# GLA layer of a two-layer trunk: gates, keys and queries projected ahead of the recurrence by the seven-product block scheme

## The chip, the cores and the metric

The kernel runs on one core of a Trainium2 chip. The metric is the device time of one execution in microseconds. The matmuls of the projections run on TensorE (PE); the other engines of the core are VectorE (DVE), ScalarE (ACT), GpSimd (POOL) and SyncE (SP), and SP's queue issues the DMAs.

## The reference

A sequence of 1024 tokens with 1024 features goes through two layers. Each has a token mixer and a SwiGLU channel mixer, both behind an RMS norm that is scaled and shifted by the conditioning vector. Layer 0 mixes by forgetting attention, layer 1 by gated linear attention (GLA), which the change is about:

```python
proj = h @ w_in                      # 1024 -> 512 q, 512 k, 1024 v, 1024 r, 16 a_lr
log_alpha = log_sigmoid(a_lr @ w_a2 + b_a) / 16
b = cumsum(log_alpha) within a chunk of 64
q_in, k_in, k_dec = q * exp(b), k * exp(-b), k * exp(b_last - b)
o_intra = tril(q_in @ k_in.T) @ v    # within the chunk
S_next = exp(b_last) * S + k_dec.T @ v
o = rms_norm(o_intra + q_in @ S) * g_o * silu(r)
y = o @ w_out
```

There are 4 heads with 128 key and 256 value features each.

## The kernel before, in words

Activations lie transposed, 128 features by 1024 tokens in a tile, in two halves of 512 tokens. A product in fp32 is three matmuls: a value is split into a rounded upper half (`split`, L163, a cast on ACT) and the rest (L164, a subtraction on DVE), and `mm3` (L241 to L243) adds upper by upper, upper by lower and lower by upper. So 128 output features of one half of the tokens cost 8 x 3 = 24 matmuls of 128x512.

The channel mixer of layer 0 doesn't multiply so. It takes weights and activations in 2 x 2 blocks and uses seven products of sums of blocks where the plain way has eight (`prod`, L1308; the sums of the products by `add`, L1317 to L1319, on DVE). Activation blocks are called B11, B12, B21, B22 and the sums T1 to T4; weight blocks are loaded and split by `op_block` and its companions (L693 and on), sums of weight blocks are made on POOL (L708, L710).

The GLA layer of before is plain. `norm_half` (L549) makes the normed activations h1. For head 0 the gate's rank-16 product and the values come first (`a_body`, `gv_body`). Then for each head `head_front` (L1693) projects keys (gk) and queries (gqp), multiplies them straight out of the matmul's accumulator by exponentials of the gate's running sum (`gate_exps`, L1675 to L1681) and splits them. `gate_ahead` (L1649) runs inside it: it makes the gate of the next head, with the scan of L1645 on DVE, and stores it in `gsum_d`. `head_back` (L1748) is the recurrence: scores in blocks (`intra`, masked at L1759 and split), the state (`state`: kv on PE, the step Sf at L1775 on DVE, its split S_t on ACT and DVE), the output go, its norm (sums of squares on ACT, L1818; gss on DVE and POOL; on_t at L1825), the transposes ogt and the product with the gate r (gs, L1788). `r_proj` (L1829) projects the head's gate r (gr, four tiles of 24 matmuls, silu at L1837 on ACT) and is woven into the recurrence. After it come the values of the next head. Heads 0 to 2 store their outputs to `og_d`; they are loaded again and split (gr, ghh, ghl), and the output product `out_chunk` (tiles go00xp) runs on them.

Weights come through one list of loads in the order of use (`feed`). Between all this `ada1` slips pieces of the conditioning product (POOL L381, ACT L379) in by a pace.

The program is written in one order, and a list scheduler with its own timeline then decides the order on each engine, by when it thinks operands and buffers ready. Names such as `weave(a, 13.0, b, 20.8)` only set the order in which it is given the work.

## Time and profile before

| what | us |
|---|---|
| three runs | 2418.40, 2418.31, 2414.46 |
| median | 2418.31 |
| profiled execution, first to last instruction (span) | 2415.5 |
| of it PE busy | 2373.4 |
| DVE busy | 1672.9 |
| ACT busy | 1191.8 |
| POOL busy | 1203.4 |

The profile tells no time of its own execution besides the span, which lies 1.0 us above the lowest and 2.9 us below the highest of the three runs. A group's row has its line, engine, operation, output and input, shapes and count, then busy time and the mean of one in ns, then the idle time of its engine just ahead of it and what ended that. A row of the timeline has start and duration, and in brackets the idle time ahead and its releaser.

### The profile page before, as it was taken

Reading aid. Unit: us, or ns where it says so; the run is one execution under the profiler, and the core shown is the slowest. Engines: PE = TensorE matmul, PEld = TensorE weight load, DVE = VectorE, ACT = ScalarE, POOL = GpSimd, SP = SyncE. Lnnn points to the kernel's source line nnn. Section 1 sums busy time; section 2 is a strip of 40 time slices with the busy share of each in tenths; the row PEclk is TensorE's granted clock in tenths of the full one; section 3 lists DMA queues with packets and bytes.
Section 4 is the critical chain, followed back from the end, with each engine's and each line's share of the span. In section 5 each row is a group of like instructions: output and inputs, shape, how many; then the busy total and the mean of one; then the engine's idle time right before and its main releaser. Section 6 shows DMA issues by size and latency. Waiting matters only on the chain.

```text
span 2415.5 us, 36053 instructions
## 1 busy us (share of the span) xinstructions
PE 2373.4 (98%) x12342; PEld 2018.3 (84%) x12342; DVE 1672.9 (69%) x2789; ACT 1191.8 (49%) x2288; POOL 1203.4 (50%) x1071
## 2 busy tenths in 40 slices
PE   7999999999999999999999999999999999999998
PEld 6788888878888888888888888898888888888888
DVE  6577677676687877876787545435586767675787
ACT  4665555675544444445324856654343333345325
POOL 4343344432347878853263646662335656653262
PEclk9999999999999999999999999999999999999999
DMA  9233333123335555457665334434325444347664
GB/s 272 72 106 114 100 111 105 62 97 114 127 103 178 184 172 174 155 187 260 228 201 171 89 110 126 135 124 154 114 85 172 164 133 151 133 174 256 232 202 148
DMA packets 329359, 361.88 MB, mean 150 GB/s; under 512 B 24460, under 2 KB 252968, under 8 KB 329176
## 3 DMA queue, kind: packets, MB, share of 16 engines
q1 hardware_dynamic: 328984, 359.57, 45.4%
q8 instruction: 97, 1.59, 0.3%
q14 instruction: 86, 0.70, 0.1%
q10 hardware_dynamic: 192, 0.02, 0.0%
HBM read 269.25 MB, written 90.24 MB: 149 GB/s over the span
## 4 chain that ended last, share of the span: by engine, by line
PE 82%; DVE 5%; DMA 4%; ACT 3%; issue 2%; POOL 2%; SPq 1%; DVEq 0%; POOLq 0%; ACTq 0%
PE p_b L243 16%; PE p_b L241 16%; PE p_b L242 16%; PE o_b L979 2%; PE t_b L965 2%; PE qk_b L241 2%; PE qk_b L243 2%; PE qk_b L242 2%; PE s_b L934 1%; PE s_b L935 1%; PE gr_b L243 1%; PE gr_b L242 1%; PE gr_b L241 1%; PE vps_b L241 1%; PE vps_b L242 1%
## 5 line engine op out<-in xcount | busy, mean ns | idle before, releaser
L164 DVE TENSOR_TENSOR o_s<-xv_s,o_s 128x512 fp32r<-128x512 f32 (+1 forms) x376 | 341.4, 911 | 78.4 <-ACT o_s L163 77.5
L163 ACT CAST o_s<-xv_s 128x512 fp32r<-128x512 f32 (+1 forms) x376 | 217.8, 587 | 320.3 <-PE p_b L243 254.4
L242 PE MATMUL p_b<-B,o_s 128*128 128x512 f32 x608 | 238.1, 392 | 0.0
L243 PE MATMUL p_b<-B,o_s 128*128 128x512 f32 x608 | 237.7, 391 | 0.0
L241 PE MATMUL p_b<-B,o_s 128*128 128x512 f32 x608 | 236.2, 391 | 0.0
L945 POOL TENSOR_SCALAR lp_s<-lp_s,st 128x128 f32<-128x128 f32 (+7 forms) x128 | 98.1, 771 | 265.7 <-DVE st L944 214.7
L708 POOL TENSOR_TENSOR ex_s<-xv_s,xv_s 128x512 f32<-128x512 f32 (+1 forms) x64 | 89.1, 1393 | 261.5 <-DMA xv_s<-in_ffn_w_in_dram 97.1
L241 PE MATMUL p_b<-T,o_s 128*128 128x512 f32 x480 | 186.7, 389 | 0.0
L242 PE MATMUL p_b<-T,o_s 128*128 128x512 f32 x480 | 186.7, 389 | 0.0
L243 PE MATMUL p_b<-T,o_s 128*128 128x512 f32 x480 | 180.7, 389 | 0.0
L243 PEld LDWEIGHTS p_b<-B,o_s 128*128 128x128 f32 x608 | 114.7, 189 | 23.9
L241 PEld LDWEIGHTS p_b<-B,o_s 128*128 128x128 f32 x608 | 114.7, 189 | 23.8
L242 PEld LDWEIGHTS p_b<-B,o_s 128*128 128x128 f32 x608 | 114.7, 189 | 23.7
L943 ACT ACTIVATE lp_s<-lp_s,st 128x128 f32<-128x128 f32 (+7 forms) x128 | 99.3, 777 | 61.1 <-DVE st L939 58.7
L381 POOL TENSOR_TENSOR ad_s<-ad_s,ad_s 128x512 f32<-128x512 f32 x62 | 89.4, 1442 | 54.0 <-ACT ad_s L379 29.6
L163 ACT CAST pt_s<-t_b 128x512 fp32r<-128x512 f32 (+1 forms) x160 | 79.6, 547 | 73.5 <-PE t_b L965 72.8
L710 POOL TENSOR_TENSOR xv_s<-ex_s,xv_s 128x512 f32<-128x512 f32 (+1 forms) x64 | 84.9, 1327 | 57.3 <-DVE o_s L164 55.1
L1319 DVE TENSOR_TENSOR ex_s<-ex_s,p_b 128x512 f32<-128x512 f32 x140 | 94.0, 680 | 27.0 <-PE p_b L243 26.9
L164 DVE TENSOR_TENSOR pt_s<-t_b,pt_s 128x512 fp32r<-128x512 f32 (+1 forms) x160 | 96.8, 631 | 13.2 <-ACT pt_s L163 12.9
L243 PEld LDWEIGHTS p_b<-T,o_s 128*128 128x128 f32 x480 | 90.1, 188 | 18.7
L241 PEld LDWEIGHTS p_b<-T,o_s 128*128 128x128 f32 x480 | 90.1, 188 | 18.7
L242 PEld LDWEIGHTS p_b<-T,o_s 128*128 128x128 f32 x480 | 90.1, 188 | 18.7
(1952 smaller groups left out, 7505.7 us busy)
## 6 DMA issues: line engine op xcount, KB each, us to landing
xv_s<-in_ffn_w_in_dram SPq DMA_DIRECT2D x176, 256.0 KB, 3.0
hid_B<-x SPq DMA_DIRECT2D x70, 512.0 KB, 2.7
ad_s<-in_ada_w_dram SPq DMA_DIRECT2D x384, 64.0 KB, 1.9
hid_T<-x SPq DMA_DIRECT2D x36, 512.0 KB, 2.8
xv_s<-in_ffn_w_out_dram SPq DMA_DIRECT2D x96, 192.0 KB, 4.1
ada_s<-in_ada_w_dram SPq DMA_DIRECT2D x128, 128.0 KB, 2.6
xv_s<-in_ffn_w_out_dram SPq DMA_DIRECT2D x40, 256.0 KB, 2.8
T2o<-hid_T SPq DMA_DIRECT2D x18, 512.0 KB, 9.0
```

The costliest lines, as they stand in the source:

```text
L163: nc.scalar.copy(hi, src)
L164: nc.vector.tensor_sub(lo, src, hi.bitcast(F32))
L241: nc.tensor.matmul(ps, ah, bh, start=start, stop=False)
L242: nc.tensor.matmul(ps, ah, bl, start=False, stop=False)
L243: nc.tensor.matmul(ps, al, bh, start=False, stop=stop)
L381: nc.gpsimd.tensor_add(acc, acc, raw)
L708: nc.gpsimd.tensor_add(s1, a21, a22)
L710: nc.gpsimd.tensor_sub(a11, s1, a11)
L943: nc.scalar.activation(lp, lp, AF.Exp, bias=mcur, scale=-1.0, accum_out=st[:, qi, 2:3])
L945: nc.gpsimd.tensor_scalar(lp, lp, st[:, qi, 3:4], 1.0, op0=ALU.mult, op1=ALU.mult)
L965: nc.tensor.transpose(tp[:, i, :], lps[qi][:, psl(2 * b + jj)], ident)
L1319: nc.vector.tensor_add(d, d if src is None else dest(G, src), ps)
```

## The change

The first layer's scheme is taken to the second layer's projections. Seven groups of two column blocks each, head 0's key and query, then for heads 1 to 3 the two gate blocks and the key and query, are projected ahead of the recurrence of all heads, each by seven products of 12 matmuls. Head 0's gate is projected plainly before them. The norm makes the blocks B and T (`g_norm`, `g_split`). A group's products are joined by `GroupRun`, one copy on ACT and seven additions on DVE; gates get their silu from SBUF; the results go to DRAM (`gs_d` for gates, `qk_d` for keys and queries). The gates' scans of all four heads run beside the groups. In the recurrence the value projection of the next head (`gv`, 64 steps of three matmuls) takes the gate's place beside `head_back`, 32 steps in it and 32 behind it; the last head has `out_chunk` there. `Front` loads running sums, keys and queries from DRAM, and multiplies and splits them; the lower halves of queries are now made on POOL. Outputs of heads 0 to 2 are loaded again ahead of head 3's recurrence.

```diff
+    GCOLS = {"r": lambda h: (2048 + 2 * h * P, 2048 + (2 * h + 1) * P),
+             "k": lambda h: (512 + h * P, h * P)}
...
+    GSEQ = [("r", 0), ("k", 0), ("r", 1), ("k", 1), ("r", 2), ("k", 2), ("r", 3), ("k", 3)]
...
-    loads += v_loads(Wg, 1024) + [(load_w16, Wg[:, 3072:3088], "aw")]
+    loads += gla_loads()
     for h in range(4):
-        if h:
-            loads += [a + (ws, 4) for a in v_loads(Wg, 1024 + h * 256)]
-        qk_ = [a + (ws, 4) for c0 in (512, 0) for a in w_loads(Wg, c0 + h * P)]
-        r_ = [a + (ws, 4) for i in range(2) for a in w_loads(Wg, 2048 + (2 * h + i) * P)]
-        loads += qk_ + r_ if h else r_[:1] + qk_ + r_[1:]
+        loads += [x_ + (ws, 4) for x_ in v_loads(Wg, 1024 + h * 256)]
...
+    y11, y21, y12, y22 = gya[:4], gya[4:], gy2[:4], gy2[4:]
+    g_block("T1", b_sl[4:8])
+    g_block("T2", b_sl[0:4])
+    g_block("T3", x_slots[0:4])
+    for k in range(4):
+        even = k % 2 == 0
+        nc.gpsimd.tensor_sub(y11[k], y12[k], y11[k])
+        g_split(gb["T1"][k], y11[k], 0)
+        nc.vector.tensor_sub(y11[k], y22[k], y11[k])
+        g_split(gb["T2"][k], y11[k], k, mcol(1, 0, k + 4) if even else None)
+    for k in range(4):
+        nc.gpsimd.tensor_sub(y12[k], y22[k], y12[k])
+        g_split(gb["T3"][k], y12[k], k, gds[:, k:k + 1] if k % 2 == 0 else None)
+    g_block("T4", hid_sl)
+    for k in range(4):
+        (nc.gpsimd if k % 2 else nc.vector).tensor_sub(y21[k], y21[k], y11[k])
+        g_split(gb["T4"][k], y21[k], 0)
...
+    def g_prod(nm_):
+
+        w, t = feed.next(), gb[nm_]
+        ps = pin([P, HALF], F32, f"gp{nm_}")
+        for k in range(4):
+            mm3(ps, w.hi[:, k, :], w.lo[:, k, :], t[k][:, 0], t[k][:, 1], k == 0, k == 3)
+        ada1(2.56)
+        return ps
...
+        OPS = ((("B11",), lambda c, p: nc.scalar.copy(c["11"], p["B11"])),
+               (("T2",), lambda c, p: nc.vector.tensor_add(c["12"], c["11"], p["T2"])),
+               (("B21",), lambda c, p: nc.vector.tensor_add(c["11"], c["11"], p["B21"])),
+               (("T3",), lambda c, p: nc.vector.tensor_add(c["22"], c["12"], p["T3"])),
+               (("T1",), lambda c, p: nc.vector.tensor_add(c["12"], c["12"], p["T1"])),
+               (("T4",), lambda c, p: nc.vector.tensor_add(c["21"], c["22"], p["T4"])),
+               (("T1",), lambda c, p: nc.vector.tensor_add(c["22"], c["22"], p["T1"])),
+               (("B22",), lambda c, p: nc.vector.tensor_add(c["12"], c["12"], p["B22"])))
+        BEFORE = {1: (0,), 2: (0, 1), 3: (1,), 4: (3,), 5: (3,), 6: (5,), 7: (3,)}
...
+    for i, gr in enumerate(GSEQ[2:]):
+        group = GroupRun(*gr)
+        group("B11", "T1")
+        if i < 4:
+            gate_ahead(i)
+        group("T2", "B21", "T3", "T4", "B22")
...
+    def gv(h, vt):
+
+        wv = [feed.next(), feed.next()]
+        for tp in range(4):
+            ps = pj([P, 2, 256], F32, f"gv{h}{tp}")
+            for i in range(2):
+                t = 2 * tp + i
+                ts_ = psl(t % 4)
+                for k in range(8):
+                    w, b_ = wv[k // 4], hb[t // 4][k]
+                    mm3(ps[:, i, :], b_[:, 0, ts_], b_[:, 1, ts_], w.hi[:, k % 4, :], w.lo[:, k % 4, :],
+                        k == 0, k == 7)
+                    yield 0.33
+            ada1(5.1)
+            v = vr([P, 2, 2, 256], FR, f"gvt{h}{tp}")
+            split(v[:, 0], v[:, 1], ps)
+            vt.append(v)
...
-            run(proj(ps, wk, h1, hf))
-            ada1(5.1)
...
-                split(t.hi[:, cs], t.lo[:, cs], y)
...
+                nc.vector.tensor_mul(y, raw[0][:, cs], ei[:, cs])
+                nc.vector.tensor_mul(t2[:, cs], raw[0][:, cs], t2[:, cs])
+                nc.scalar.copy(kin.hi[:, cs], y)
+                nc.gpsimd.tensor_sub(kin.lo[:, cs], y, kin.hi[:, cs].bitcast(F32))
...
+                for t, f in zip(qt, (ei, b16)):
+                    y = yv()
+                    nc.vector.scalar_tensor_tensor(y, raw[1][:, cs], QS, f[:, cs], op0=ALU.mult, op1=ALU.mult)
+                    nc.scalar.copy(t.hi[:, cs], y)
+                    nc.gpsimd.tensor_sub(t.lo[:, cs], y, t.hi[:, cs].bitcast(F32))
+                yield
...
-            yield from proj(ps, wr_[dv], h1, hf)
-            ada1(5.1)
-            nc.scalar.activation(gs[dv][:, hsl(hf)], ps, AF.Silu)
-            done.add((dv, hf))
...
-        weave(head_back(h, kin, qt, kd, t2, dec, vt, gs, need), 13.0, rg, 20.8)
...
+        gs = load_gs(h)
         if h < 3:
-            with tc.issue_after(sq_ins[0]):
-                b16, t2, ei, dec = gate_exps(h + 1, gnext.pop())
-            wv = [feed.next(), feed.next()]
-            vt = [gv_body(h + 1, wv, 0)]
-            head_end(h, gs)
-            vt += [gv_body(h + 1, wv, tp) for tp in range(1, 4)]
-            head_store(h, gs)
-            pj = Ring(psp, list(own.q) + list(opr.q))
-
-
-    ada1.flush()
-    oh = new_h("gh")
-    for k in range(6):
-        reload_h(og_d, oh, k, "gr")
+            vn, nxt = [], Front(h + 1)
+            g = gv(h + 1, vn)
+            fs = nxt.steps()
+            weave(head_back(front, vt, gs), 13.0, beside(part_of(g, 32), fs, {8, 16, 24}), 10.6)
+            run(head_end(h, gs))
+            run(beside(g, fs, {0, 6, 12, 18, 24}))
+            run(fs)
+            vt, front = vn, nxt
+        else:
+            oh_sl = H_SL[:12] + hid_sl
+            x_slots = to_sl[0:2] + b_sl[1:3] + H_SL[12:16]
+            oh = [Pair(big.tile([P, S], FR, tag=oh_sl[2 * k], name=f"ghh{k}"),
+                       big.tile([P, S], FR, tag=oh_sl[2 * k + 1], name=f"ghl{k}")) for k in range(6)]
+            for k in range(6):
+                reload_h(og_d, oh, k, "gr")
+            ada1.flush()
+            xs = [big.tile([P, S], F32, tag=x_slots[k], name=f"x1_{k}") for k in range(8)]
+            for k in range(8):
+                nc.sync.dma_start(xs[k], x_d[k])
+            first = out_chunk(0, 4, oh, xs, 1, 2, "go", (0, 1))
+            weave(head_back(front, vt, gs), 13.0, first, 43.0)
+            run(head_end(3, gs))
```

How the order on the engines changes, at three places. First PE before, in head 2's recurrence, with numbers by head: kv23 is the state's product for head 2, gr201 a tile of its gate, go201 its output.

```order
7701 L241 MATMUL kv23_b4_18_15455<-gvt21_s49_10_14966,kdh2_s30_11_15260 128x256
7702 L242 MATMUL kv23_b4_18_15455<-gvt21_s49_10_14966,kdh2_s30_11_15260 128x256
7703 L243 MATMUL kv23_b4_18_15455<-gvt21_s49_10_14966,kdl2_s42_12_15261 128x256
7704 L241 MATMUL gr201_b0_19_15521<-h1h3_12686,w2560_h_s24_114_15095 128x512
7705 L242 MATMUL gr201_b0_19_15521<-h1l3_12687,w2560_h_s24_114_15095 128x512
7706 L241 MATMUL go201_b6_10_15441<-gvt21_s49_10_14966,ahl20_s52_5_15328 128x256
7707 L242 MATMUL go201_b6_10_15441<-gvt21_s49_10_14966,ahl20_s52_5_15328 128x256
7708 L243 MATMUL go201_b6_10_15441<-gvt21_s49_10_14966,ahl20_s52_5_15328 128x256
7709 L241 MATMUL go201_b6_10_15441<-S_t_12977,gq21h_s34_11_15221 128x256
7710 L243 MATMUL gr201_b0_19_15521<-h1h3_12686,w2560_l_s45_115_15096 128x512
```

The gate's matmuls stand in every gap between the state's and the output's. PE after, in the same recurrence of head 2, from the end of kv22 to the start of kv24:

```order
8053 L243 MATMUL kv22_b4_17_16004<-gvt21_s36_10_15724,kdl2_s30_6_15854 128x256
8054 L241 MATMUL go200_b5_9_15969<-S_t_14472,gq21h_s50_11_15789 128x256
8055 L242 MATMUL go200_b5_9_15969<-S_t_14472,gq21h_s50_11_15789 128x256
8056 L243 MATMUL go200_b5_9_15969<-S_t_14472,gq21l_s51_12_15790 128x256
8057 L241 MATMUL kv23_b4_18_16034<-gvt21_s36_10_15724,kdh2_s29_5_15853 128x256
8058 L242 MATMUL kv23_b4_18_16034<-gvt21_s36_10_15724,kdh2_s29_5_15853 128x256
8059 L243 MATMUL kv23_b4_18_16034<-gvt21_s36_10_15724,kdl2_s30_6_15854 128x256
8060 L241 MATMUL go201_b6_10_16020<-S_t_14472,gq21h_s50_11_15789 128x256
8061 L242 MATMUL go201_b6_10_16020<-S_t_14472,gq21h_s50_11_15789 128x256
8062 L243 MATMUL go201_b6_10_16020<-S_t_14472,gq21l_s51_12_15790 128x256
8063 L241 MATMUL kv24_b4_19_16055<-gvt22_s41_11_15816,kdh2_s29_5_15853 128x256
```

The gate's matmuls of 128x512 between kv23, go201 and kv24 are gone from here, and the steps of the recurrence stand next to each other; the next rows of another kind are the output tiles go000p.

On DVE, before, at the start of head 0's recurrence: b16a_1 and t2a_1 are head 1's gate, gq head 0's queries, atz and ahl00 the masked scores.

```order
1743 L1642 TENSOR_TENSOR t2a_1_s42_2_13554<-b16a_1_s30_1_13553,t2a_1_s42_2_13554 128x1024
1744 L1645 SCALAR_TENSOR_TENSOR b16a_1_s30_1_13553<-rm_12971,t2a_1_s42_2_13554 128x512 x2
1745 L164 TENSOR_TENSOR gq01l_s27_4_13515<-gy_s35_12967,gq01h_s34_3_13514 128x512
1746 L164 TENSOR_TENSOR gq00l_s33_2_13513<-gy_s35_12967,gq00h_s32_1_13512 128x512
1747 L1759 COPY_PREDICATED atz_s37_12968<-tri_84,at00_b3_1_13623 128x512
1748 L1722 SCALAR_TENSOR_TENSOR gy_s35_12967<-gqp01_b2_15_13565,b16_0_s41_1_13146 128x512
1749 L164 TENSOR_TENSOR ahl00_s52_1_13637<-atz_s37_12968,ahl00_s52_1_13637 128x512
```

After, the scans stand among the additions of the groups, far ahead of the first scores. The third place is DVE in head 3's recurrence of after: Sf and S_t are its state, ghl4 and ghl5 the outputs of head 2 that were loaded again, x1 the residual that takes an output tile.

```order
2023 L164 TENSOR_TENSOR ghl4_16447<-gr4_s18_105_16466,ghh4_16446 128x1024
2024 L164 TENSOR_TENSOR S_t_14472<-Sf31_16618,S_t_14472 128x256
2025 L2015 TENSOR_SCALAR gss300_16602<-gss300_16602 128x2
2026 L164 TENSOR_TENSOR S_t_14472<-Sf32_16660,S_t_14472 128x256
2027 L1972 SCALAR_TENSOR_TENSOR Sf33_16701<-Sf32_16660,dec3_16110,kv33_b4_25_16697 128x256
2028 L2018 TENSOR_SCALAR on_t_14473<-go300_b5_13_16601,gss300_16602 128x256 x2
2029 L1972 SCALAR_TENSOR_TENSOR Sf34_16735<-Sf33_16701,dec3_16110,kv34_b4_26_16731 128x256
2030 L164 TENSOR_TENSOR ghl5_16449<-gr5_s16_106_16470,ghh5_16448 128x1024
2031 L164 TENSOR_TENSOR S_t_14472<-Sf33_16701,S_t_14472 128x256
2032 L1123 SCALAR_TENSOR_TENSOR x1_2_16507<-go020p_b0_22_16649,modc_167,x1_2_16507 128x512
```

Before, the splits ghl0 to ghl5 stand on DVE among the last two steps of head 3's state, Sf35 and Sf36, and the additions to x1 come behind them all; after, ghl0 to ghl3 are in head 2's recurrence, ghl4 and ghl5 stand between the first steps of head 3's state, and additions to x1 come among these rows.

471 lines of the change are left out of this document (273 added, 198 removed).

## The prediction

> **What bounds the kernel now.** I read the page first, for the span, TensorE's share and the chain that ended last; then the windows around the second layer's mixer, for the stages with gaps in them; then the waits of PE and the timeline there, for the price of one matmul and of one stall; and last the groups of instructions on DVE, for what the new order puts close together.
>
> ```profile
> span 2415.5 us, 36053 instructions
> PE 2373.4 (98%) x12342; PEld 2018.3 (84%) x12342; DVE 1672.9 (69%) x2789; ACT 1191.8 (49%) x2288; POOL 1203.4 (50%) x1071
> PE 82%; DVE 5%; DMA 4%; ACT 3%; issue 2%; POOL 2%; SPq 1%; DVEq 0%; POOLq 0%; ACTq 0%
> ```
>
> TensorE is busy 98% of the span and makes up 82% of the chain that ended last. A matmul that goes shortens the kernel by its own pitch, as long as PE is still the engine that is waited for. The columns of the windows are start:end, length, then busy time and instructions of PE, PE's weight loads, DVE, ACT and POOL, then the granted clock and the DMA share.
>
> ```profile
> 700.00:1290.00 590.00, 589.19 (x2601) 487.19 (x2601) 459.65 (x571) 247.87 (x440) 365.71 (x250) 1.00 0.56 189
> 1325.40:1380.00 54.60, 54.13 (x304) 47.24 (x304) 27.20 (x39) 43.91 (x83) 31.32 (x31) 1.00 0.31 87
> 1380.00:1393.60 13.60, 11.53 (x62) 9.46 (x61) 10.58 (x11) 7.84 (x12) 10.13 (x8) 1.00 0.58 175
> 1393.60:1403.90 10.30, 9.81 (x35) 8.56 (x34) 4.64 (x9) 6.12 (x12) 6.58 (x7) 0.50 0.51 154
> 1403.90:1682.00 278.10, 277.06 (x1696) 247.42 (x1696) 135.16 (x224) 158.90 (x341) 143.73 (x146) 1.00 0.41 129
> ```
>
> The first row is the bulk of the first layer's channel mixer, which already runs the seven-product scheme: PE has 0.8 us of idle in 590. The last row holds nearly all four heads of the recurrence, with gates, keys and queries projected beside it: 1.0 us of idle in 278, with DVE at 49%. So that stage is filled to the brim, and DVE has half its time free because a projection always stands between two steps of the recurrence. The rows between them are the one bad place: head 0's start, with 2.1 us of idle and then 10.3 us at half clock.
>
> **The matmuls removed.** The pitch is read from starts, since the ends are modelled: first 128x512, then 128x256.
>
> ```profile
> 1530.22 0.39 PE L241 MATMUL gk_b<-h1h,w_h_s 128*128 128x512 f32 x1
> 1530.45 0.39 PE L242 MATMUL gk_b<-h1l,w_h_s 128*128 128x512 f32 x1
> 1530.67 0.39 PE L243 MATMUL gk_b<-h1h,w_l_s 128*128 128x512 f32 x1
> ```
>
> ```profile
> 1413.72 0.28 PE L241 MATMUL gv_b<-wv_0h_s,h1h 128*128 128x256 f32 x1
> 1413.84 0.28 PE L242 MATMUL gv_b<-wv_0l_s,h1h 128*128 128x256 f32 x1
> 1413.96 0.28 PE L243 MATMUL gv_b<-wv_0h_s,h1l 128*128 128x256 f32 x1
> ```
>
> That is 0.227 us and 0.12 us. Before, one column block of 128 takes 48 matmuls of 128x512, so a pair of blocks takes 96; a group of seven products with 12 each takes 84. The change puts seven pairs (k0, r1, k1, r2, k2, r3, k3) into groups: 7 x 12 = 84 matmuls fewer, 84 x 0.227 = **-19.1 us**. Values, gates of rank 16, recurrence and output keep their matmuls. The order has this count (8090 of 128x512 before, 8006 now), so the rival that the change does not do what it says is out.
>
> **What the groups add.** Per group seven weight blocks are split on ACT and DVE, and the products are joined by one copy on ACT and seven adds on DVE. The nearest rows are those of the same work in the channel mixer:
>
> ```profile
> L164 DVE TENSOR_TENSOR o_s<-xv_s,o_s 128x512 fp32r<-128x512 f32 (+1 forms) x376 | 341.4, 911 | 78.4 <-ACT o_s L163 77.5
> L1319 DVE TENSOR_TENSOR ex_s<-ex_s,p_b 128x512 f32<-128x512 f32 x140 | 94.0, 680 | 27.0 <-PE p_b L243 26.9
> ```
>
> 7 x 0.911 + 7 x 0.680 = 11.1 us of DVE against 84 x 0.227 = 19.1 us of PE per group. I add nothing for this stage: the window 700 to 1290 carries DVE at 78% beside the same products without an idle PE. The cover that hides it is the products themselves. The sixteen tiles of 512 KB that go to DRAM and come back (16 MB) are spread over more than 300 us, with the DMA engines at 31 to 58% in the windows above; they are asked for a head ahead, so I take zero, and name their waits as a sign below.
>
> **Head 0's start.** The timeline of DVE at that place, and the row of PE that waited:
>
> ```profile
> 1385.32 3.26 DVE L1645 TENSOR_TENSOR_SCAN b16a_s<-rm,t2a_s 128x512 f32<-128x512 bf16 x2
> 1388.51 1.16 DVE L164 TENSOR_TENSOR gq01l_s<-gy_s,gq01h_s 128x512 fp32r<-128x512 f32 x1
> 1389.59 1.22 DVE L164 TENSOR_TENSOR gq00l_s<-gy_s,gq00h_s 128x512 fp32r<-128x512 f32 x1
> 1390.74 0.71 DVE L1759 COPY_PREDICATED atz_s<-tri,at_b 128x512 f32<-128x512 int32 x1
> ```
>
> ```profile
> 1392.15 0.39 PE L241 MATMUL go_b<-gvt_s,ahl_s 128*128 128x256 f32 x1 [1.97 <-ACT ahl_s L163]
> ```
>
> The waits of PE from 1300 to 1700, the longest two:
>
> ```profile
> PE go_b L241 <- ACT ahl_s L163: 2.0, 1, 2.0
> PE go_b L243 <- DVE ahl_s L164: 0.8, 1, 0.8
> ```
>
> The masking of the first scores stands in DVE's queue behind the scan of head 1's gate and two subtractions, so PE waits 1.97 us; then the clock is at 0.50 for 10.3 us. At full clock its 35 recorded matmuls would take at most 35 x 0.227 = 7.9 us, and at least half of the busy 9.81: between 2.4 and 5.4 us of the 10.3 are lost, I take 4.2. With the two waits on the masked scores, 2.0 and 0.8 us, that is **-7 us**, as the change moves the scans into the product stage (3.3 us beside a group's 11.1 of DVE, under 19.1). It could be zero, if another wait starts the same slow spell there.
>
> **The recurrences of heads 2 and 3.** Here the change costs. In the new order the last value projection (gv33) is used up while head 2 has only just begun. Up to kv36 there are then, counted in the order, 72 matmuls of 128x512 (the six output tiles), 101 of 128x256 and 50 transposes and score blocks: 72 x 0.227 + 151 x 0.12 = 34.4 us of PE, the small ones taken at the pitch of 128x256. Before, head 3 alone had 96 gate matmuls (21.8 us) beside it and head 2 as many again. On DVE the same stretch holds 76 rows. Their prices, by the groups on DVE from 1300 to 1690:
>
> ```profile
> L164 DVE TENSOR_TENSOR S_t<-Sf,S_t 128x256 fp32r<-128x256 f32 x28 | 15.6, 559 | 10.3 <-ACT S_t L163 10.3
> L1825 DVE TENSOR_SCALAR on_t<-go_b,gss 128x256 f32<-128x256 f32 x32 | 14.0, 478 | 10.6 <-POOL gss L1823 7.4 <-PE ogt_b L1785 3.2
> L1788 DVE SCALAR_TENSOR_TENSOR gs_s<-ogt_b,vec,gs_s 128x512 f32<-128x512 f32 x16 | 12.0, 748 | 12.0 <-PE ogt_b L1785 11.7
> L1775 DVE SCALAR_TENSOR_TENSOR Sf<-Sf,dec,kv_b 128x256 f32<-128x256 f32 x24 | 11.5, 477 | 25.9 <-PE kv_b L243 25.9
> L164 DVE TENSOR_TENSOR gvt_s<-gv_b,gvt_s 128x512 fp32r<-128x512 f32 x16 | 10.9, 687 | 28.2 <-ACT gvt_s L163 28.2
> L164 DVE TENSOR_TENSOR ghl<-gr_s,ghh 128x1024 fp32r<-128x1024 f32 x6 | 7.3, 1222 | 2.3 <-ACT ghh L163 2.2
> L164 DVE TENSOR_TENSOR ahl_s<-atz_s,ahl_s 128x512 fp32r<-128x512 f32 x8 | 6.0, 756 | 1.9 <-ACT ahl_s L163 1.7
> L1822 DVE TENSOR_SCALAR gss<-gss 128x2 f32<-128x2 f32 x16 | 2.8, 178 | 11.6 <-ACT mib L1818 11.6
> ```
>
> Of the DMA issues:
>
> ```profile
> gr_s<-og_d SPq DMA_DIRECT2D x6, 512.0 KB, 4.0
> ```
>
> 14 Sf (6.7), 12 S_t (6.7), 12 on_t (5.7), 3 ghl (3.7), 3 gvt (2.1), 3 ahl (2.3), 6 gss (1.1), and 23 rows of 128x512 or half of it at 0.68 to 0.75 (4 gs, 6 additions to x, 3 splits of decayed keys, 2 masks, 4 of head 3's keys and queries, 2 of weights, 2 small ones: about 15.7): 44 us. A step of the state cannot be compressed either: kv's three matmuls, Sf 0.48, the cast on ACT, S_t 0.56, then go. With the 4.0 us reload of head 2's outputs ahead of ghl4 and ghl5, which the S_t rows stand behind, I arrive by hand at 46 us for the 34.4 of PE: **+12 us** idle. The low end: if DVE and ACT have run ahead, only single waits as the two of head 0's start are left, some 3 us. The clock adds to it. The row 1393.60 shows 10.3 us at half clock after one wait of 1.97; here waits of 1 to 2 us come one after another, and I take **+3 us**, for a spell whose matmuls are sparse, so that most of the slower work falls into waits. The high end is the second rival.
>
> [...]
>
> **Heads 0 and 1, and the start.** Keys, queries and values of heads 0 and 1 still have gv of the next head beside them (192 x 0.12 = 23 us a head, before 96 x 0.227 = 21.8 of gates). But 16 subtractions of queries move from DVE to POOL, and the scaled keys and queries are now made from SBUF tiles instead of PSUM:
>
> ```profile
> L164 DVE TENSOR_TENSOR gq10l_s<-gy_s,gq10h_s 128x512 fp32r<-128x512 f32 x2 | 3.4, 1710 | 3.3 <-ACT gq10h_s L163 3.3
> L164 DVE TENSOR_TENSOR gq31l_s<-gy_s,gq31h_s 128x512 fp32r<-128x512 f32 x2 | 1.4, 678 | 0.0
> L1707 POOL TENSOR_TENSOR kil_s<-gy_s,kih_s 128x512 fp32r<-128x512 f32 x8 | 11.7, 1464 | 2.3 <-ACT kih_s L1706 2.3
> ```
>
> On POOL one takes 1.46 us, and the two gy buffers let DVE's next product wait for it; PE waits where that is later than the gv filler lasts. Bounds 0 and 13 us, the second if each of a head's four waits 0.8 us; I take **+3**. At the start of the product stage POOL makes 16 differences and lower halves before the T3 blocks are whole, 16 x 1.46 = 23.4 us, while PE has two gate tiles, the rank-16 tiles and three products from the second norm on (48 + 32 + 36 matmuls at 0.227, 26 us): close, **+2** between 0 and 5.
>
> **Sum.** -19.1 - 7 + 12 + 3 + 3 + 2 = -6.1 us. The profiled span is 2415.5; the runs' times are 2414.46, 2418.31 and 2418.4, so it lies within them, and I take the sum off the median: 2418.3 - 6.1 = **2412 us**. 0.2%, about what a measurement of this kernel can tell from no change, is 4.8 us; below 2413.5 is faster, above 2423.1 slower.
>
> **The rivals.** *The recurrences stay covered.* For it: the window 1403.90 has 142 us of DVE time free. Then only 3 or 4 us of waits are left there, and 0 to 5 in the other two places: -26.1 + 3 to 9, so 2395 to 2401; chance 0.25. *The clock stays down.* The other side, in the stretch from gv33 to kv36 the waits keep PE at 0.50, as the single one did in the row 1393.60, and the 34.4 us of work take 68.8, with PE the slowest again. That is +34.4 in place of +15: 2418.3 - 26.1 + 34.4 + 5 = 2432. It decides, against no change, from 26 us lost in the stretch. Against it: in the last row of the windows the clock is 1.00 across all small waits. Chance 0.2. *POOL and DVE hold each other up.* The same subtraction takes 678 ns on DVE in one head and 1710 in another. If the 32 products of keys and queries that now read two SBUF tiles are drawn out by half a us each while POOL works, and DVE is 16 us longer with 10 of them on the path, the heads cost 13 instead of 3: 2422, no change; chance 0.15. [...]
>
> **How the numbers follow.** Chances: forecast 0.4 (2405 to 2419), covered recurrences 0.25, low clock 0.2, POOL 0.15. Faster: 0.25 from the covered case and 0.27 of the forecast's 0.4, 0.52; same: 0.13 of the forecast and 0.11 of POOL's, 0.24; slower: the low clock and the rest, 0.24. The range from 2396 to 2429 leaves out the end of the first rival and the upper half of the low clock, under 2 in 10. The forecast's own range is 2405 to 2419.
>
> **What would show it.** Right: the product stage at under 1 us of idle per 100, no spell at 0.50 at head 0's first go, and in the windows of heads 2 and 3 some 34 us of PE work in 45 to 50 with Sf, S_t, ahl or ghl as what PE waits for. Wrong: a second pass of heads 2 and 3 without idle (first rival), with PEclk 0.50 throughout (second), or waits of PE on kil, gq or gy in heads 0 and 1 of over 10 us (third). If the product stage itself shows idle, the step that took it as covered has failed.

## The result and the profile after

The changed kernel takes 2446.58 us (median of 4 runs, 2444.20 to 2450.14) against 2416.39 us of the kernel before on the same chips (2412.16 to 2418.40): a ratio of 1.0126, with a 95% interval from 1.0110 to 1.0142. It is 30 us slower, where 6 us faster was forecast. The page of the changed kernel, first lines:

```profile
span 2444.8 us, 36223 instructions
PE 2374.1 (97%) x12258; PEld 2014.4 (82%) x12258; DVE 1776.1 (73%) x2886; ACT 1209.8 (49%) x2325; POOL 1254.8 (51%) x1069
```

84 matmuls are gone, as counted, and DVE has 103 us more to do. The windows of the changed kernel show where the time went; the columns are those of the prediction's windows.

```profile
700.00:1290.00 590.00, 589.84 (x2606) 488.29 (x2605) 460.28 (x575) 248.81 (x441) 366.35 (x250) 1.00 0.58 191
1309.90:1513.00 203.10, 184.27 (x782) 148.43 (x781) 153.76 (x168) 120.12 (x194) 137.28 (x92) 0.93 0.49 153
1513.00:1640.00 127.00, 123.57 (x1027) 122.14 (x1026) 81.98 (x129) 82.05 (x209) 84.34 (x80) 1.00 0.47 144
1640.00:1704.00 64.00, 52.55 (x250) 44.16 (x249) 43.55 (x76) 31.74 (x76) 29.58 (x26) 0.76 0.63 212
1704.00:1780.00 76.00, 76.00 (x359) 63.37 (x358) 47.50 (x72) 29.05 (x55) 27.98 (x31) 1.00 0.35 111
```

The first layer's channel mixer is as before. The product stage (second row) has 18.8 us of idle PE at a mean clock of 0.93; heads 0 and 1 (third row) lose 3.4 us; the recurrences of heads 2 and 3 (fourth) have 11.5 us of idle in 64 at a clock of 0.76; then PE is full again. What PE waited for from 1310 to 1760, the longest sums:

```profile
PE grp_b L242 <- POOL gB L1605: 8.0, 2, 7.4
PE gpT_b L241 <- DVE gr_s L1741: 4.1, 1, 4.1
PE kv_b L241 <- DVE Sf L1970: 3.6, 3, 2.1
PE gpT_b L241 <- DVE gk_s L1741: 2.7, 1, 2.7
PE go_b L241 <- ACT mib L2012: 2.2, 1, 2.2
```

So two places fail, about equally. The longest wait is for a lower half of a B block on POOL. POOL's timeline there:

```profile
1351.15 6.09 POOL L1672 TENSOR_TENSOR te_s<-te_s,te_s 128x512 f32<-128x512 f32 x1 [4.24 <-DVE te_s L1665]
1357.20 1.70 POOL L1605 TENSOR_TENSOR gB<-gy_s,gB 128x512 fp32r<-128x512 f32 x1
```

The half (L1605) stands behind a subtraction for T4 (L1672), which waits 4.2 us for DVE and then takes 6.1 us, where another of its kind at 1358.87 takes 1.72. The waits on a group's additions (L1741) come from ACT's queue:

```profile
1395.21 1.27 ACT L1783 ACTIVATE t2a_s<-z_b,vec 128x512 f32<-128x512 f32 x2 [4.52 <-DVE b16a_s L1796]
1396.49 1.28 ACT L1791 ACT_TABLE_LOAD   x1
1397.79 1.06 ACT L1791 ACTIVATE t2a_s<-t2a_s 128x1024 f32<-128x1024 f32 x1
1398.87 1.28 ACT L1792 ACT_TABLE_LOAD   x1
1400.16 1.06 ACT L1792 ACTIVATE t2a_s<-t2a_s 128x1024 f32<-128x1024 f32 x1
1401.12 0.60 ACT L163 CAST o1k_s<-xv_s 128x512 fp32r<-128x512 f32 x1
```

A gate waits 4.5 us for the scan of the gate before it, since there is one pair of gate tiles, and then takes 6 us with its function tables; the cast of the weight block (o1k_s) comes only after it. DVE waits 2.3 us for that cast, and the addition stands behind it in DVE's queue. The second of these waits, 2.7 us at 1426.87, comes from a conditioning piece: ACT stands 3.5 us before the piece's row of weights, and the copy with which the group's additions begin (L1740) is behind it.

```profile
1424.26 0.72 ACT L379 ACTIVATE ad_s<-ad_s,cblk 128x512 f32<-128x512 f32 x1 [3.47 <-DMA ad_s<-in_ada_w_dram]
...
1425.40 0.58 ACT L1740 COPY gk_s<-gpB_b 128x512 f32<-128x512 f32 x1
```

Over the product stage (1310 to 1513) ACT stands 30.3 us before such rows, and in the same stretch of before (1311.5 to 1513) 8.7 us:

```profile
ACT ad_s L379 <- DMA ad_s<-in_ada_w_dram: 30.3, 14, 4.5
```

```profile
ACT ad_s L379 <- DMA ad_s<-in_ada_w_dram: 8.7, 6, 3.2
```

### The profile page after: what moved, and what is told of

It reads as the page before. It is cut to its first block, busy times and chain, and to the rows that moved or that the text cites. A ratio compares the mean times of both kernels' runs of the same rounds, so it can differ in the third digit from the quotient of the medians.

```text
span 2444.8 us, 36223 instructions
## 1 busy us (share of the span) xinstructions
PE 2374.1 (97%) x12258; PEld 2014.4 (82%) x12258; DVE 1776.1 (73%) x2886; ACT 1209.8 (49%) x2325; POOL 1254.8 (51%) x1069
## 4 chain that ended last, share of the span: by engine, by line
PE 82%; DVE 6%; DMA 4%; issue 2%; POOL 2%; ACT 2%; SPq 1%; POOLq 0%; DVEq 0%; ACTq 0%
PE p_b L243 16%; PE p_b L242 16%; PE p_b L241 16%; PE o_b L1028 2%; PE t_b L1014 2%; PE qk_b L241 2%; PE qk_b L242 2%; PE qk_b L243 2%; PE s_b L983 1%; PE s_b L984 1%; PE vps_b L241 1%; PE vps_b L242 1%; PE vps_b L243 1%; SPq L361 1%; DMA ad_s<-in_ada_w_dram 1%
## 5 line engine op out<-in xcount | busy, mean ns | idle before, releaser
L713 POOL TENSOR_TENSOR ex_s<-xv_s,xv_s 128x512 f32<-128x512 f32 (+1 forms) x70 | 98.1, 1401 | 269.1 <-DMA xv_s<-in_ffn_w_in_dram 95.4
L715 POOL TENSOR_TENSOR xv_s<-ex_s,xv_s 128x512 f32<-128x512 f32 (+1 forms) x70 | 95.5, 1365 | 67.9 <-DVE o_s L164 55.8
L725 POOL TENSOR_TENSOR xv_s<-xv_s,xv_s 128x512 f32<-128x512 f32 x46 | 65.1, 1416 | 82.4 <-issue 63.3
L242 PEld LDWEIGHTS p_b<-T,o_s 128*128 128x128 f32 x480 | 90.1, 188 | 18.7
L241 PEld LDWEIGHTS p_b<-T,o_s 128*128 128x128 f32 x480 | 90.1, 188 | 18.7
```

The source lines that it names most:

```text
L241: nc.tensor.matmul(ps, ah, bh, start=start, stop=False)
L242: nc.tensor.matmul(ps, ah, bl, start=False, stop=False)
L713: nc.gpsimd.tensor_add(s1, a21, a22)
L715: nc.gpsimd.tensor_sub(a11, s1, a11)
L725: nc.gpsimd.tensor_sub(r[A12], r[A12], r[A11])
```

## The experiments

Single times of one kernel scatter by some us (the kernel before lies between 2412 and 2422), and the layer begins between 1309.6 and 1316.1 us in runs that do the same work ahead of it. So the runs are compared by a stage: from the start of the last matmul of the first layer's last output tile (f0e11871p) to that of the mixer's last output tile in the second layer (go1471p). I call it the layer; the first value matmul parts it into a product stage and the rest. In the kernel before the layer takes 439.2 us (1311.4 to 1750.6), in the changed one 470.5:

```profile
1309.56 0.39 PE L243 MATMUL f0e11871p_b<-hh,oo_s 128*128 128x512 f32 x1
...
1780.09 0.39 PE L243 MATMUL go1471p_b<-ghh,wo_768l_s 128*128 128x512 f32 x1
```

That is +31.3, against +30.2 of the medians. Five runs whose edits lie behind the product stage or touch it only by the order (after, late, gvhold, noreload, junk) have it at 203.4, 204.2, 204.6, 206.9 and 208.0 us, so a difference of under 5 us is not read. The kernel's time is a median of four runs for before, after, best1, best2 and best3, and one run for each of the others.

| run | product stage | rest | layer | kernel |
|---|---|---|---|---|
| before | | | 439.2 | 2416.4 |
| after | 203.4 | 267.1 | 470.5 | 2446.6 |
| t4dve | 206.7 | 263.9 | 470.6 | 2446.2 |
| alldve | 206.6 | 266.8 | 473.4 | 2454.0 |
| spread | 210.5 | 266.1 | 476.6 | 2458.3 |
| late | 204.2 | 263.4 | 467.6 | 2446.7 |
| onegate | 193.1 | 262.9 | 456.0 | 2436.2 |
| noada | 190.1 | 316.3 | 506.4 | 2487.4 |
| k0plain | 200.6 | 265.4 | 466.0 | 2442.9 |
| k0r1plain | 203.4 | 271.6 | 475.0 | 2452.7 |
| junk | 208.0 | 281.4 | 489.4 | 2466.2 |
| depth5 | 202.2 | 268.7 | 470.9 | 2449.2 |
| adapace | 195.9 | 276.6 | 472.5 | 2449.1 |
| best1 | 182.9 | 282.3 | 465.2 | 2443.1 |
| noreload | 206.9 | 258.0 | 464.9 | 2443.3 |
| gvhold | 204.6 | 266.0 | 470.6 | 2447.7 |
| best2 | 184.3 | 262.9 | 447.2 | 2449.1 |
| best3 | 185.1 | 281.4 | 466.5 | 2443.6 |
| lean1 | 185.2 | 248.0 | 433.2 | 2410.7 |
| lean2 | 186.8 | 247.4 | 434.2 | 2415.0 |

**One wait at a time.** Theory: each of the waits has its own cause in the order of a queue. Rival: the engines beside PE are too full, and what is freed at one place is waited for at the next.

```diff
-        (nc.gpsimd if k % 2 else nc.vector).tensor_sub(y21[k], y21[k], y11[k])
+        nc.vector.tensor_sub(y21[k], y21[k], y11[k])
```

> The two subtractions for T4 that stood on POOL go to DVE; nothing else changes. Theory 1 (order of POOL's queue): the wait of 7.4 us of the gate tile on the lower half of a B block came because that half stood on POOL behind a T4 subtraction, which itself waited 4.2 us for DVE and then took 6.1 us. Without it the wait falls under 2 us, the half clock behind it goes, and the span falls by 8 to 11 us. Rival (DVE and POOL together are too slow for this stretch): PE waits 4 us or more for some other block between 1340 and 1370, and the span falls by under 5 us.

The wait for the lower half fell from 8.0 to 0.6 us, and the stage did not get shorter. The waits of PE in this run:

```profile
PE gpB_b L243 <- DVE o1k_s L164: 7.6, 3, 3.9
PE gpT_b L241 <- ACT o1r_s L163: 3.6, 1, 3.6
PE gpT_b L241 <- ACT o1k_s L163: 3.3, 1, 3.3
```

They are for splits of weight blocks now. The span did not fall, as the rival said; the wait of 4 us or more that it named for some other block between 1340 and 1370 came out at 3.3 us.

```diff
-            (nc.gpsimd if k % 2 else nc.vector).tensor_sub(lo, y, hi.bitcast(F32))
+            (nc.gpsimd if k % 2 and not ssm else nc.vector).tensor_sub(lo, y, hi.bitcast(F32))
...
-        nc.gpsimd.tensor_sub(y11[k], y12[k], y11[k])
+        nc.vector.tensor_sub(y11[k], y12[k], y11[k])
```

> All of the second half's norm and the T blocks goes to DVE, 18 instructions more of 128x512 there and none on POOL. Theory (an instruction of POOL and one of DVE that read two tiles keep each other waiting): the mean of DVE's lower halves of B and T falls from 1.2 us or more to about 0.7 us, DVE's stretch from the norm to the last T block stays within 5 us of its 33 us although it has 18 instructions more, and PE's longest wait falls under 4 us. Rival (DVE is simply full): durations stay, DVE's stretch grows by 18 x 0.68 = 12 us, and PE waits 10 us or more.

DVE's groups from 1325 to 1375, first of the changed kernel, then of this one:

```profile
L1605 DVE TENSOR_TENSOR gT<-te_s,gT 128x512 fp32r<-128x512 f32 x8 | 7.8, 978 | 2.0 <-ACT gT L1604 1.8
L1602 DVE SCALAR_TENSOR_TENSOR gB<-gy_s,modc,gB 128x512 fp32r<-128x512 f32 x4 | 6.7, 1689 | 0.0
```

```profile
L1605 DVE TENSOR_TENSOR gT<-te_s,gT 128x512 fp32r<-128x512 f32 x9 | 5.8, 677 | 0.0
L1602 DVE SCALAR_TENSOR_TENSOR gB<-gy_s,modc,gB 128x512 fp32r<-128x512 f32 x4 | 3.0, 749 | 0.0
```

With POOL's share of this work gone the same instruction falls from 1689 to 749 ns. The stretch from the norm (L1611) to the last T block (L1605) takes 45.8 us in place of 40.2 with 18 instructions more: 5.6 us, a little over the 5 of the theory of mutual blocking and half of the rival's 12. PE's longest wait in it is 3.4 us. So two of three numbers go with the theory and the third lies near it. Still the layer gains nothing, which the expectation hadn't asked: further on PE waits 6.8 us at once for ACT's cast of a weight block.

```diff
-        if i < 4:
-            gate_ahead(i)
+        if i in {0: 0, 2: 1, 4: 2, 5: 3}:
+            gate_ahead({0: 0, 2: 1, 4: 2, 5: 3}[i])
```

> The gates of the four heads are put beside the groups r1, r2, r3 and k3 (positions 0, 2, 4, 5) instead of r1, k1, r2, k2. Theory (one pair of gate tiles, and the chain Abs, Exp, Ln, scan in ACT's and DVE's queues holds up the weight splits and the additions): the waits of 4.1 and 2.7 us on the groups' additions near 1404 and 1427 go, with their slow clock, and the span falls by 7 to 11 us; a wait may be left at the last two gates, which are still next to each other. Rival (the groups' own work on DVE is too much): waits on the additions of 5 us or more in sum stay, and the span stays within 3 us.

It missed: 4.1 us on the additions stayed, 6.3 us for a cast of a weight block came, and the stage is 7 us longer. Putting the gates apart does not help.

**What the product stage has too much of.**

```diff
-            gate_ahead(i)
+            if i:
+                nc.sync.dma_start(gsum_d[i], b0)
+            else:
+                b0 = gate_ahead(i)
```

> Leaves work out: only head 0's gate is made beside the groups, and its running sum is stored for all four heads. Theory (the product stage is bound by what ACT, DVE and POOL do in it, the gates being the part that the first layer's channel mixer hasn't got): three gates are some 20 us of DVE and 20 of ACT less, and the stage from the last output tile of the first layer to the first value matmul falls from 203 us by 10 to 16. Rival (the norm's blocks and T blocks at its start set the whole delay, and the gates only take the waits over): it falls by under 4 us.

10.3 us shorter: the gates are a part.

```diff
         w, t = feed.next(), gb[nm_]
...
-        ada1(2.56)
```

> The pieces of the conditioning product (one ACT, one POOL instruction each) are no longer slipped in beside the groups but later, in the recurrence; the result is the same. Theory (POOL's work draws DVE's out, and ACT's queue holds up the weight splits): the product stage falls by 4 to 10 us from 203; the recurrence may lose some of it. Rival (they fill free time only): under 2 us.

13.3 us shorter, more than expected. Most of the pieces then ran at the output tiles, which wait for them (PE 31.0 us at once for a piece on POOL; 96 us from head 3's last transpose to the end of the first half's output, 13.5 in the changed kernel), so the rest of this run says nothing.

```diff
-    GSEQ = [("r", 0), ("k", 0), ...
+    NPL = 1    # groups behind r0 that are projected plainly
```

> Group k0 is projected plainly: 12 matmuls more (2.7 us), 7 additions on DVE and 4 sums on POOL less, three weight blocks less to split, and some 19 us more of plain matmuls before the first T block is needed. Theory (the start is bound by the preparation of B and T blocks on DVE and POOL, which has no cover): the product stage falls by 8 to 14 us net. Rival (gates and weight splits bound it all the way): it rises by 0 to 3 us.

The edit puts k0's four blocks through the tile loop of head 0's gate; only its count of groups is shown. 2.8 us shorter with 2.7 us of matmuls more. That is not the 8 to 14 us of the theory of the start, and too little to read against its rival's 0 to 3 us more.

```diff
-    NPL = 1
+    NPL = 2
```

> Groups k0 and r1 are projected plainly: 24 matmuls more (5.4 us) than in the changed kernel. Theory of the start: as k0 alone, the cover is enough after the first group, so 1 to 4 us longer than k0 alone. Rival (the whole stage is bound by DVE, ACT and POOL): every plain group takes 11 us off DVE, and this one is shorter than k0 alone by 5 us or more.

It is not 5 us shorter than k0 alone, as its rival asks, but 2.8 us longer. That speaks against the rival; the 1 to 4 us of the theory are within the scatter.

```diff
+    feed.depth = 5
     wg = [[None, None], [None, None]]
```

> Weight blocks of the product stage are asked for five ahead, as in the first layer's channel mixer, instead of three. Theory (weights are prepared too late because so few are in flight): the product stage falls by 5 us or more from 203. Rival (ACT, DVE and POOL are full, asking earlier doesn't help): within 3 us.

1.2 us shorter, within the scatter: no help from asking earlier is seen.

**Moving the conditioning pieces.**

```diff
-        ada1(2.56)
+        ada1(0.8)
...
-            ada1(5.1)
+            ada1(6.5)
...
+            first = out_chunk(0, 4, oh, xs, 1, 2, "go", (0, 1), before=ada_m)   # ada_m(m): ada1(7.0)
```

> The conditioning product's 62 pieces are paced otherwise: about 11 beside the groups, 30 in the recurrences and the rest beside the output tiles. From the run without any beside the groups (190 us) theory gives a product stage of 192 to 195 us and recurrences up to 4 us longer, the whole layer 5 to 9 us shorter than 470. Rival (in the recurrences they cost as much as beside the groups): within 3 us.

The product stage won 7.5 us and the rest lost 9.5: the rival.

```diff
+    NPL = 1
...
+    feed.depth = 5
...
+        ada1(0.8)
```

> All that helped so far in one: k0 plain, weights five ahead, the other pace of the conditioning pieces, head 1's outputs reloaded later. If the gains add up (4.5 + 3 + 7 + 3 us), the layer takes 450 to 456 us and the kernel about 2425 to 2432 us, still slower than before. If DVE and ACT merely pass the delay on, 462 us or more and about 2440.

It joins k0plain, depth5, late and adapace. The product stage is at 182.9 us, PE waits there nowhere but once at its start; the rest is 15 us longer. 2443.10 us (ratio 1.0110, 1.0093 to 1.0126): the second case.

```diff
-        ada1_queue((0,), v[0], v[1:4])
+        ada1_queue((0, 2), v[0], v[1:4])
-    ADA_A, ADA_B = 6.0, 3.0
+    ADA_A, ADA_B = 3.0, 1.5
```

> k0 plain, weights five ahead, head 1's outputs split later, and half of the conditioning pieces moved into the first layer's channel mixer, where DVE, ACT and POOL have room; none beside the groups. If that room is free, the product stage takes 180 to 184 us as in the run of all gains, the rest some 263 to 267, the layer 445 to 450, and the kernel about 2420 to 2426 us. If the pieces cost as much there, the first layer is longer by 5 us or more.

The layer is at 447.2 as expected, but it begins at 1334.5 us, where in all other runs it begins between 1309.6 and 1316.1 us: 31 pieces more beside the first layer's seven-product stage cost some 20 us. A window of this run:

```profile
600.00:1310.00 710.00, 696.13 (x3101) 573.14 (x3100) 533.24 (x682) 311.61 (x551) 444.46 (x315) 0.99 0.57 185
```

DVE is at 75% and POOL at 63%, with PE idle for 14 us. That this stage had no room either is not shown: at the doubled pace ACT stood 38.4 us before the pieces' rows (window 600 to 1334), where the 31 pieces of the changed kernel never waited for one.

```profile
ACT ad_s L379 <- DMA ad_s<-in_ada_w_dram: 38.4, 12, 6.1
```

The kernel takes 2449.13 us (1.0127, 1.0099 to 1.0156).

**The recurrences of heads 2 and 3.** Theory: too few matmuls beside them. Rivals: reloads in ACT's and DVE's queues; the chain itself.

```diff
+                if 1 < k < 4:
+                    es.enter_context(tc.issue_after(st_ins[2, 3]))   # ACT's cast of head 2's fourth state
                 reload_h(og_d, oh, k, "gr")
```

> The reload and split of head 1's outputs (gr2, gr3) are put behind the fourth state step of head 2. Theory (ACT's queue stands 5.5 us before the reload and with it the splits of head 2's recurrence): the wait of 2.1 us of kv on the first Sf and the slow clock from 1645 to 1659 go, and the stretch from gv33 to head 3's last kv is shorter by 6 to 10 us. Rival (the stretch is bound by DVE's 76 rows, whichever comes first): the idle comes back later in the stretch, and its length changes by under 3 us.

The time lost to the slow clock in this stretch (PE's busy time times what the clock lacked of 1.00, summed over windows of 2 us) fell from 12.8 to 5.5 us, the wait of kv on the first Sf from 2.1 to 1.1, and the stage after the first value matmul by 3.7, within the scatter: unclear.

```diff
             st["S"] = Sn
+            if h >= 2:
+                jk = pj([P, HALF], F32, f"jk{h}{n}")
+                with tc.issue_after(last_of("P")):
+                    for i in range(6):
+                        nc.tensor.matmul(jk, kd.hi[:, n, :], kin.hi[:, 0:HALF], start=i == 0, stop=i == 5)
```

> Adds 84 matmuls of 128x512 (19 us at 0.227) that nobody reads, six behind each state step of heads 2 and 3, as a stand-in for the gate tiles that stood there before. Theory (these recurrences have too little PE work beside their steps, and the clock is low because of the gaps): PE no longer waits 2 us at a time there, the clock stays at 1.00 from 1640 to 1720, and the stage from the first value matmul to the end of the mixer's output (267 us) grows by less than 6 us, so 13 or more of the 19 fall into time that was lost anyway. Rival (the gaps are not there for want of work, each chain waits on DVE, ACT or DMA whatever PE does): it grows by 15 to 19 us and the low clock stays.

The rest grew by 14.3 us, near the rival: only 5 of the 19 us fell into lost time. The rest's loss to the slow clock fell from 12.8 to 8.8 us, so it did not stay as the rival had it, nor go as the theory had it.

```diff
+                for x_, n_ in (((2, 2), 8), ((2, 4), 8), ((2, 6), 17)):
+                    for _ in range(n_):
+                        with tc.issue_after(kv_ins[x_]):
+                            c_ = next(held_g, None)
```

> The last two of head 3's four value tiles (96 matmuls of 128x256, 11.5 us) are held back on PE and put between the state steps of head 2, where before they ran ahead of head 2's first step; no work is added or left out. Theory (the matmuls that should lie beside the steps are used up too early): the slow clock from 1640 on falls to half and the stage of 267 us is shorter by 5 to 10 us. Rival (the time only moves: PE now waits earlier, while head 2's keys are prepared): within 3 us.

266.0 for 267.1: the time only moved. The rest's loss to the slow clock did fall to about half (12.8 to 6.9 us), but PE's idle time in it rose from 14.9 to 19.0. The theory that the matmuls are used up too early falls.

```diff
-            for k in range(6):
-                reload_h(og_d, oh, k, "gr")
+            oh = [front.kin] * 6
```

> Leaves work out: the outputs of heads 0 to 2 are not loaded again and split; the output tiles read head 3's keys in their place, as many matmuls as before. Theory (ACT and DVE stand before reloads that come late, and with them the steps of the state): the stage from the first value matmul to the end of the mixer's output falls by 8 us or more from 267. Rival (the chain of the state itself is too long for the work beside it): by under 4 us.

9.1 us shorter. In the changed kernel ACT's groups from 1640 to 1704 have these two that wait for loads:

```profile
L379 ACT ACTIVATE ad_s<-ad_s,cblk 128x512 f32<-128x512 f32 x10 | 7.2, 721 | 9.7 <-DMA ad_s<-in_ada_w_dram 9.7
L163 ACT CAST ghh<-gr_s 128x1024 fp32r<-128x1024 f32 x4 | 4.2, 1045 | 7.0 <-DMA gr_s<-og_d 7.0
```

ACT stands 9.7 us for the conditioning's rows and 7.0 for the reloads in these 64 us, and everything of the state's steps that is cast on ACT stands behind. So the pieces were left out too:

```diff
-        steps = deque(range(0, 32, n))
+        top = 2 if l and j else 32
+        steps = deque(range(0, top, n))
```

> Leaves work out: of the conditioning pieces of the second layer's last two pairs, 2 of 32 each are made. Otherwise k0 plain, weights five ahead, head 1's outputs split later. Theory (ACT and POOL instructions between the steps, and ACT's waits for their loads, delay the recurrence): product stage 180 to 184 us, the rest of the layer 250 to 258 instead of 267, the layer 432 to 442. Rival (the pieces cost only beside the groups): the rest stays at 263 to 267, the layer at 445 to 450.

It has k0plain, depth5 and late as well. Layer 433.2 us, 6 us under the kernel before; the rest 248.0.

```diff
-            for k in range(6):
-                reload_h(og_d, oh, k, "gr")
+            oh = [front.kin] * 6
```

> As lean1, and the outputs of heads 0 to 2 are not loaded again (output tiles read head 3's keys). If reloads and pieces are separate costs, another 8 to 10 us go and the rest of the layer is about 243 to 250 us; what stays above the 232 us of its matmuls at full pitch is then the chain of the state. If they delay the same steps, under 4 us go.

247.4 us: the reloads cost nothing that can be read once the pieces are gone, so both delay the same steps.

```diff
-        ada1(2.56)
+        ada1(0.8)
...
-            ada1(5.1)
+            ada1(9.0)
```

> Computes everything: k0 plain, weights five ahead, head 1's outputs split later, about 11 of the 62 conditioning pieces beside the groups and the rest beside the value projections. Product stage 182 to 185 us, the rest 267 to 272, the layer 450 to 456, the kernel 2424 to 2432 us: faster than the changed kernel, still slower than before. If the pieces cost 0.4 us each in the recurrence as they do beside the groups, the rest is 275 us or more and nothing is won over 2440.

The counterpart of lean1 that computes everything. The product stage is as long (185.1), the rest is 281.4 us, the kernel 2443.59 us (1.0101, 1.0082 to 1.0120): its second case. No version found that computes everything beats the kernel before. The groups of DVE over the layer in lean1, then in best3:

```profile
L2035 DVE TENSOR_SCALAR on_t<-go_b,gss 128x256 f32<-128x256 f32 x32 | 14.0, 478 | 11.2 <-PE ogt_b L1999 5.6 <-POOL gss L2033 5.5
L164 DVE TENSOR_TENSOR S_t<-Sf,S_t 128x256 fp32r<-128x256 f32 x28 | 13.0, 463 | 4.9 <-ACT S_t L163 4.6
```

```profile
L164 DVE TENSOR_TENSOR S_t<-Sf,S_t 128x256 fp32r<-128x256 f32 x28 | 22.2, 795 | 6.7 <-ACT S_t L163 6.5
...
L2034 DVE TENSOR_SCALAR on_t<-go_b,gss 128x256 f32<-128x256 f32 x32 | 14.0, 478 | 6.6 <-PE ogt_b L1998 3.6 <-POOL gss L2032 2.9
```

With 60 instructions of POOL more, the split of the state takes 795 ns instead of 463, 28 times on the state's chain, 9.3 us; in the kernel before, which makes all pieces, it took 559. ACT stands 44.4 us before the pieces' rows in the rest of best3's layer, and never in lean1; on_t, which reads the accumulator of the matmuls and one column of numbers, takes 478 in both.

## Why the prediction was wrong

- **The matmuls.** Right in the count: 84 fewer, 19.1 us at their pitch (see the sum below).
- **What the groups add.** This step failed. It put the product stage at zero, with 2 us for its start, because the first layer's stage carries DVE at 78% without an idle PE. The product stage has DVE at 76% and lost 18.8 us idle and 10.0 us of clock (by the sum over windows of 2 us). So the busy share at which one stage held was no measure of room in another. And the sum had no term for what was to run beside the groups: the conditioning pieces are not in it at all, although the trace of before had 62 of them in this layer, and the gates were dismissed by DVE's 3.3 us of scan, without ACT's chain with its tables. The runs without them give 13.3 and 10.3 us.
- **Head 0's start.** Right: that stall and its slow clock are gone, the clock is 1.00 from 1513 to 1640.
- **Heads 2 and 3.** The idle time came out as forecast, 11.5 us for 12, but in part by luck. It was priced by DVE's rows and one reload against too few matmuls; holding matmuls back for these steps changed nothing, and added ones cost 14 of 19 us. The steps were late for work that is not in that price, or not enough: ACT stood 9.7 us before the pieces' rows, which it leaves out, and 7.0 before reloads, of which it has one of 4.0; and the state's splits took 0.62 us on the mean, where lean1 without the pieces has 0.46. Two kernels that differ in the 60 pieces and their pace differ by 33.4 us in the rest of the layer (281.4 and 248.0), and the reloads add nothing to that.
- **The clock there.** 12.8 us for 3: the term was of the right kind and four times too small, since the clock, each of the eight times that it went low, stayed low for one to four windows of 3.41 us (below). Part of it falls into waits, as forecast: in late it shrank by 7.3 us and the stage by 3.7.
- **Heads 0 and 1.** Right: 3.4 us for 3.
- **The rivals.** The low clock is part of the loss, but not through the whole stretch: it was 0.76 there, not 0.50. POOL and DVE holding each other up was the nearest, though not with its price: 16 of the 32 products that it named were drawn out as it said (L1918, 1.21 and 1.09 us for 0.68 before), but heads 0 and 1 lost only 3.4 us, and the blocks at the start (1.69 us, in alldve 0.75), the weight splits there (o1k_s, 1.47 us, in alldve 0.95) and the state's split (0.62 us, in lean1 0.46) were drawn out too.

The terms as they came out: -19.1 - 7 + 28.8 + 3.4 + 24.3 = +30.4, for a layer that is 31.3 us longer. That this closes so well is luck, since -19.1 and -7 are the forecast's own. Taken by one measure over the layer, PE's idle time and slow clock were 4.5 and 6.6 us before and are 33.7 and 22.8 us now, 45.4 more; so the rest of PE's time fell by 14.1 us and not by 19.1. Where these 5 us are is open.

What makes the pieces dear now and not before is argued, not shown: no run took them out of the kernel before, and no run parts ACT's waits for their rows from what DVE's instructions lose beside POOL's. The sums over the layer, from windows that cover it (PE, its weight loads, DVE, ACT, POOL), of before, of the changed kernel and of lean1:

```profile
sum 439.10, PE 434.43 PEld 382.52 DVE 224.01 ACT 246.88 POOL 222.86; mean PE 108.61 PEld 95.63 DVE 56.00 ACT 61.72 POOL 55.71
```

```profile
sum 470.50, PE 436.79 PEld 378.43 DVE 327.19 ACT 263.25 POOL 279.47; mean PE 109.20 PEld 94.61 DVE 81.80 ACT 65.81 POOL 69.87
```

```profile
sum 433.20, PE 421.33 PEld 369.15 DVE 286.85 ACT 227.69 POOL 180.90; mean PE 105.33 PEld 92.29 DVE 71.71 ACT 56.92 POOL 45.22
```

DVE was busy for 51% of the layer before and for 70% after, POOL for 51 and 59. The projections that were thinned out had been PE time beside which all this was done; the change took 19 us of it away and put 103 us on DVE.

## What to carry to other kernels

Busy shares did not tell here what room a stage has: with DVE at 78% PE was idle for 0.2 us in 590 in the first layer's channel mixer, with DVE at 76% for 18.8 in 203 in the product stage. Before work is moved beside such a stage, put a little of it there and measure, rather than adding up busy shares. When a change removes filler from PE, list all that ran beside it, above all work of other parts of the program that is slipped in by a pace, and price it at the new place with its queue, including the time that a queue may stand before a load (here 30.3 us of ACT in the product stage). And an instruction's price may depend on what runs beside it (on DVE 1.69 us beside POOL's half of the norm's blocks and 0.75 without it), so look at one instruction's duration with and without the neighbour.

## What the runs showed of the hardware

**In the changed kernel the clock went low on a grid of 3.41 us.** The granted clock goes low at 1320.47, 1354.60, 1402.39, 1426.28, 1457.00, 1644.73, 1678.87 and 1689.11 us; all distances are whole multiples of 3.413. Windows cut on that grid:

```profile
1398.97:1402.39 3.42, 1.27 (x4) 0.47 (x4) 1.12 (x3) 3.41 (x5) 0.00 (x0) 1.00 0.33 98
1402.39:1405.80 3.41, 1.47 (x3) 0.99 (x4) 3.41 (x5) 1.53 (x4) 2.12 (x1) 0.50 0.02 5
1405.80:1409.21 3.41, 3.41 (x9) 2.64 (x9) 3.41 (x6) 2.19 (x4) 0.00 (x0) 0.50 0.26 105
1409.21:1412.63 3.42, 3.42 (x16) 2.77 (x16) 3.42 (x7) 3.39 (x5) 1.65 (x2) 1.00 0.51 161
```

```profile
1542.33:1545.75 3.42, 1.85 (x14) 1.44 (x12) 1.02 (x2) 3.42 (x8) 3.08 (x5) 1.00 0.17 48
1545.75:1549.16 3.41, 3.34 (x28) 3.31 (x29) 3.20 (x5) 3.41 (x12) 3.39 (x4) 1.00 0.52 154
```

```profile
1641.32:1644.73 3.41, 1.78 (x17) 1.64 (x15) 1.14 (x2) 2.22 (x4) 0.58 (x1) 1.00 0.41 167
1644.73:1648.15 3.42, 2.63 (x11) 2.37 (x11) 3.42 (x8) 3.08 (x10) 1.21 (x1) 0.50 0.99 346
1648.15:1651.56 3.41, 3.41 (x15) 2.97 (x14) 1.59 (x3) 2.69 (x5) 0.00 (x0) 0.50 1.03 419
1651.56:1654.97 3.41, 2.33 (x8) 1.65 (x8) 3.21 (x9) 2.22 (x8) 1.49 (x2) 0.50 1.03 398
```

```profile
1685.69:1689.11 3.42, 2.00 (x13) 1.37 (x12) 1.23 (x3) 1.32 (x3) 0.00 (x0) 1.00 1.00 343
1317.05:1320.47 3.42, 3.35 (x30) 3.35 (x31) 1.69 (x2) 0.00 (x0) 2.41 (x2) 1.00 0.11 46
```

Behind a window in which PE was busy for 1.27 us the next one was slow, and so it was behind one with 1.78; behind one with 1.85 it was not. Busy time alone gives no sharp border here: the window from 1685.69 has 2.00 us and the next one is slow, and so is the one behind 1317.05, which is busy for 3.35 us, by their records, with 30 matmuls of 128x1. The clock came back behind a well-filled window (1405.80), but one was not always enough: the window from 1648.15 is full and the next is still slow, and from 1644.73 to 1658.39 it is four windows. At 0.50 matmuls of 128x512 started 0.43 us apart (1407.18 and 1407.61), at 1.00 0.23 (1410.21 and 1410.44). By the 0.50 a slow window full of matmuls costs 1.7 us, half of its 3.41, so the one to four windows behind a wait are estimated at 1.7 to 6.8 us.

**Instructions of DVE took longer beside POOL's.** An instruction of DVE on two 128x512 tiles of SBUF (L1602) took 1.69 us on the mean beside POOL's half of the same work and 0.75 without it (alldve); the state's split of 128x256 took 0.80 with the 60 pieces (best3) and 0.46 without them (lean1). One instruction of POOL (L1672) took 6.09 us while DVE was busy without a break, the next of its kind 1.72. An instruction of DVE that reads the matmuls' accumulator (on_t) took 0.48 us with the pieces and without. Why instructions are drawn out so no run shows.
